# Where the activation buffers of a one-core decoder trunk begin, and a down projection in three passes

## The chip, the cores and the metric

One core of one Trainium2 chip runs the whole program. The metric is the device time of one execution in microseconds (us), taken as the median of several runs. The program has one launch and no communication with other cores.

## The reference

One decoder layer on 256 tokens of width 2048, in float32, with modulation vectors that come from a conditioning vector `c`. Cut to what matters:

```python
mod = silu(c) @ w_ada + b_ada                 # w_ada 2048 x 12288
sh1, sc1, g1, sh2, sc2, g2 = split(mod, 6)
h = rms_norm(x, norm_mix) * (1 + sc1) + sh1
proj = h @ w_in                               # "in":   2048 x 6656
mixed = concat(retention(proj), rwkv7(proj), moba_attention(proj))
x = x + g1 * (mixed @ w_out)                  # "out":  2048 x 2048
h = rms_norm(x, norm_ffn) * (1 + sc2) + sh2
u = causal_conv3(h @ w_up)                    # "up":   2048 x 11264
val, gate = split(u, 2)
x = x + g2 * ((silu(gate) * val) @ w_down)    # "down": 5632 x 2048
return rms_norm(x, norm_final)
```

The three mixers take little time beside the four projections; what bears on the change is the projections.

## The kernel before, in words

**Tiles and passes.** Activations lie transposed: features on the 128 partitions, the 256 tokens along the free dimension. Each float32 operand of a projection is split in two parts, `hi` (rounded to float32r) and `lo` (the rest). For each weight tile of 128 x 128 and each input tile of 128 features (a `k`), TensorE adds `whi*hi`, `whi*lo` and `wlo*hi` into a PSUM tile; the weight tile is the stationary operand and the activations are the moving one. "in", "out" and "up" do this in three passes of 256 columns (L1209, L1210, L1211). "down" (`WIDE`) does it in two: `whi` against `[hi | lo]` side by side, 512 columns into a whole PSUM bank (L1204), then `wlo*hi`, 256 columns into its first half (L1206). `evac_down` then adds both halves of the bank to the residual `x` (L1143, two operations).

**Counts.** A k of one output tile is one triplet of passes (a pair in "down"). "in" has 52 output tiles x 16 k = 832 triplets, "out" 16 x 16 = 256, "up" 88 x 16 = 1408, "down" 16 x 44 = 704. Of "up", 64 triplets (the first four k of 16 output tiles) run early, from `xg` (L1072 to L1082, 258 columns), while the norm before the MLP is still unknown, and are scaled by it later (L1095). The other 1344 triplets, 4032 matmuls, run from the normalized tiles `h` (L443 to L453).

**Weights.** SP's queue brings 1 MB (or 2 x 512 KB) `raw` buffers. Each holds two chunks of 8 weight tiles. ScalarE casts a chunk to `hi` (L471), VectorE subtracts to `lo` (L472), each of 128 x 1024. There are three buffers of each (`CONVB`), and `convert_until` runs two chunks ahead of the matmuls (`AHEAD`). Between the weights VectorE multiplies and sums 96 blocks of `w_ada` (L419, 128 x 2048 each), from the same raw buffers.

**Order.** The order of the weight tiles is a table (`weight_order`). The main loop goes over chunks: convert, hooks, eight triplets, evacuations, and some steps of the mixers' generators. A scheduler decides how the instructions that belong to different chunks are interleaved on each engine.

**The norm before "up".** After the last output tile of "out", the sum of squares (`acc`, L1061) goes through a matmul (`nps`, L1065), a short chain on VectorE that forms 1/sqrt by Newton steps (L385, L242 to L247, each on 128 x 2), a matmul that spreads it to all partitions (`rs`, L389) and a copy on ScalarE (`rs_ffn`, L399). With it the `h` tiles of "up" can be made. The last stretch of the kernel does the same with the final norm.

**Where buffers begin.** Activations that feed TensorE lie in the `arena` pool, 30 buffers of one tag. One buffer is `4T + 4` = 1028 floats, 4112 bytes, which the allocator rounds to 4128, and the pool begins at byte 31,104 of a partition. So the n-th buffer begins at 31104 + 4128 n, that is 384 + 32 n modulo 512: sixteen different places modulo 512. `pairs` puts hi and lo of two k into one buffer. The six converted weight buffers all begin at 320 modulo 512. These addresses are those of the built program.

```python
def piece(dt, name):                                              # L204
    return arena.tile([128, 4 * T + 4], dt, tag="s4", name=name)
```

Of the kernel before, what the change touches and what calls it, by code (L numbers as in the profile page):

```python
# [12 lines left out]
OP = mybir.AluOpType  # L13
# [155 lines left out]
WIDE = ("down",)  # L169
# [4 lines left out]
def trunk(tc, A):  # L174
# [254 lines left out]
    def split(g, sl, src):  # L429

        if g not in MX:
            MX[g] = pairs("mx")
        f, n, ts = sl
        while n:
            w = min(n, 2 - f % 2)
            x = MX[g][f // 2][:, f % 2:f % 2 + w]
            hi, lo = x[:, :, 0, ts], x[:, :, 1, ts]
            S.copy(hi, src[:, 0:w])
            V.tensor_tensor(lo, src[:, 0:w], hi.bitcast(F32), op=OP.subtract)
            src = src[:, w:]  # L440
            f, n = f + w, n - w

    def h_tile(kind, f):  # L443

        g, j = f // 4, f % 4
        if g not in H:
            H[g] = pairs("h")
        hi, lo = (H[g][j // 2][:, j % 2, i] for i in range(2))
        gain, shift = (mod[kind + n][:, f:f + 1] for n in ("_gain", "_shift"))
        xn = small.tile([128, T], F32, tag="xn", name=nm("xn"), bufs=2)  # L450
        V.scalar_tensor_tensor(xn, XN[kind][g][:, j], gain, RS[kind], op0=OP.mult, op1=OP.mult)
        S.activation(hi, xn, AF.Identity, bias=shift)
        V.scalar_tensor_tensor(lo, xn, shift, hi.bitcast(F32), op0=OP.add, op1=OP.subtract)  # L453
# [6 lines left out]
    def convert_until(c):  # L460
        while len(chunks) <= c and pos[0] < len(stream_items):
# [59 lines left out]
    def retention():  # L521
# [44 lines left out]
        for hh in range(2):  # L566
# [7 lines left out]
            split(0, (2 * hh, 2, slice(0, T)), mixed[:, 2 * hh:2 * hh + 2])  # L574
# [4 lines left out]
    def moba(h):  # L579
# [43 lines left out]
        split(g, (h % 4, 1, slice(0, T)), o[:, None, 0:256])  # L623
# [5 lines left out]
    def rwkv():  # L629
# [88 lines left out]
        R = [eighth(f"R{h}") for h in range(2)]  # L718
        vT, bT, kT = (half(n) for n in ("vT", "bT", "kT"))
# [61 lines left out]
        YV = half("yv")  # L781
# [78 lines left out]
        bd = [eighth(f"bd{h}") for h in range(2)]  # L860
# [49 lines left out]
        U = half("U")  # L910
# [4 lines left out]
        for h in range(2):  # L915
# [80 lines left out]
            split(1, (0, 4, sl), mixed[:, :, sl])  # L996
# [106 lines left out]
    def evac_up(t, part, ps):  # L1103
# [51 lines left out]
    def operands(m, k):  # L1155
# [3 lines left out]
        return src[k // 4][k % 4 // 2][:, k % 2]  # L1159
# [15 lines left out]
    for c in range(n_chunks):  # L1175
# [5 lines left out]
        for j in range(8):  # L1181
# [16 lines left out]
            ps = opened[t] if m in WIDE else opened[t][:, 0:T + 2] if early else opened[t][:, 0:T]  # L1198
            two = t in both
            opens = first and not (two and t % 2)  # L1200
# [96 lines left out]
```

## Time and profile before

| what | us |
|---|---|
| median of 3 runs | 1322.31 (1319.69 to 1325.14) |
| profiled execution, its own time | 1320.23 |
| span of its trace | 1318.3 |
| PE busy | 1269.5 (96%) |
| VectorE (DVE) busy | 1040.2 (79%) |
| ScalarE (ACT) busy | 651.1 (49%) |
| GpSimd (POOL) busy | 43.7 (3%) |
| mean granted TensorE clock | 0.987 |

The difference between the execution's own time and its span (1.9 us) is what lies outside the first and last instruction. A matmul of 256 columns is recorded with some 0.28 us, of which the larger part overlaps the next one; what a matmul costs in a row of them is the distance from its start to the start of the next, called its **pitch** below. It is read from the starts in the timeline, or from the length of a stretch and the count of matmuls in it. The stages, by the matmuls' lines: "in" 23 to 396.5 us, "out" 396.5 to 541.3, the early part of "up" to 583.3, "up" to 1057.0, "down" to 1302.7, the final norm and the last stores to 1318.4.

### The profile page before, as it was taken

What the parts mean: (1) busy time and instruction counts of PE and PEld (TensorE: products, weight loads), DVE (VectorE), ACT (ScalarE), POOL (GpSimd) and SP (SyncE); (2) the same over time, 40 slices, a digit from 0 to 9 for tenths busy, and PEclk for the clock granted to TensorE, in tenths of its full rate; (3) what the DMA queues carried; (4) which work ended last, traced back from release to release, by engine and by line L of the source; (5) the groups of instructions that cost most, each with busy time, mean ns of one, the idle gap of its engine ahead of it and who ended that gap; (6) DMA issues with size and microseconds to landing.
All of it is one profiled execution on the core that took longest, in us unless ns stands there. A gap on an engine that the chain in (4) does not pass through costs nothing.

```text
span 1318.3 us, 23905 instructions
## 1 busy us (share of the span) xinstructions
PE 1269.5 (96%) x9820; PEld 1219.6 (93%) x9820; DVE 1040.2 (79%) x1624; ACT 651.1 (49%) x1045; POOL 43.7 (3%) x41
## 2 busy tenths in 40 slices
PE   5899999999999999979999999999999999999995
PEld 5899999999999999979999999999999988888885
DVE  7888989999887579998776888898866766666544
ACT  3455445666345324456555656566555544444441
POOL 0000000000000001400000000000000000100000
PEclk8999999999999999989999999999999999999998
DMA  9999887785537269695864565565555666767551
GB/s 387 359 328 349 315 311 290 280 290 192 208 123 277 96 248 409 236 341 204 307 240 158 192 220 196 181 215 184 219 193 193 219 248 247 283 251 278 198 192 64
DMA packets 49934, 320.48 MB, mean 243 GB/s; under 512 B 5536, under 2 KB 6048, under 8 KB 15776
## 3 DMA queue, kind: packets, MB, share of 16 engines
q1 hardware_dynamic: 48528, 315.10, 65.1%
q0 software_dynamic: 1008, 3.67, 0.7%
q8 instruction: 77, 1.26, 0.4%
q14 instruction: 33, 0.27, 0.1%
q10 hardware_dynamic: 288, 0.17, 0.1%
HBM read 316.83 MB, written 2.10 MB: 242 GB/s over the span
## 4 chain that ended last, share of the span: by engine, by line
PE 55%; DVE 1%; ACT 0%; DVEq 0%; issue 0%; ACTq 0%
PE mm L1204 12%; PE mm L1209 12%; PE mm L1211 12%; PE mm L1210 12%; PE mm L1206 6%; DVE x L1151 0%; PE rs L389 0%; DVE x L1143 0%; DVEq L1292 0%; PE ms L1065 0%; DVE rsa L246 0%; DVE rsy L247 0%; DVE rsa L245 0%; DVE acc L1061 0%; ACT nsq L1060 0%
## 5 line engine op out<-in xcount | busy, mean ns | idle before, releaser
L472 DVE TENSOR_TENSOR lo<-raw,hi 128x1024 fp32r<-128x1024 f32 x400 | 489.2, 1225 | 194.7 <-ACT hi L471 192.5
L471 ACT CAST hi<-raw 128x1024 fp32r<-128x1024 f32 x400 | 419.5, 1050 | 436.7 <-PE mm L1210 248.3
L1209 PE MATMUL mm<-h,hi 128*128 128x256 f32 x2016 | 567.4, 282 | 0.7 <-ACT hi L471 0.6
L1211 PE MATMUL mm<-h,lo 128*128 128x256 f32 x2016 | 566.2, 281 | 1.1 <-DVE lo L472 1.1
L1210 PE MATMUL mm<-h,hi 128*128 128x256 f32 x2016 | 566.6, 281 | 0.0
L1211 PEld LDWEIGHTS mm<-h,lo 128*128 128x128 f32 x2016 | 379.9, 189 | 2.2 <-DVE lo L472 1.5
L1209 PEld LDWEIGHTS mm<-h,hi 128*128 128x128 f32 x2016 | 379.9, 188 | 1.8 <-ACT hi L471 0.8
L1210 PEld LDWEIGHTS mm<-h,hi 128*128 128x128 f32 x2016 | 379.7, 188 | 0.3
L1204 PE MATMUL mm<-g,hi 128*128 128x512 f32 x704 | 245.9, 394 | 0.0
L419 DVE SCALAR_TENSOR_TENSOR raw<-raw,cb 128x2048 f32<-128x2048 f32 x96 | 220.9, 2301 | 3.5 <-DMA raw<-w_ada 3.1
L1206 PE MATMUL mm<-g,lo 128*128 128x256 f32 x704 | 197.5, 281 | 0.0
L1204 PEld LDWEIGHTS mm<-g,hi 128*128 128x128 f32 x704 | 132.2, 188 | 30.3
L1206 PEld LDWEIGHTS mm<-g,lo 128*128 128x128 f32 x704 | 132.7, 188 | 0.0
L1209 PE MATMUL mm<-mx,hi 128*128 128x256 f32 x256 | 73.5, 287 | 1.2 <-DVE x L1047 1.2
L1210 PE MATMUL mm<-mx,hi 128*128 128x256 f32 x256 | 72.9, 285 | 0.0
L1211 PE MATMUL mm<-mx,lo 128*128 128x256 f32 x256 | 72.0, 281 | 0.5 <-DVE lo L472 0.5
L1061 POOL TENSOR_TENSOR acc<-acc,nsq 128x256 f32<-128x256 f32 x28 | 37.7, 1345 | 837.1 <-ACT nsq L1060 836.7
L1209 PE MATMUL pair<-h,hi 128*128 128x256 f32 x160 | 45.5, 296 | 7.0 <-ACT hi L471 5.1
L1209 PEld LDWEIGHTS mm<-mx,hi 128*128 128x128 f32 x256 | 48.2, 188 | 2.3 <-DVE x L1047 1.4
L1211 PEld LDWEIGHTS mm<-mx,lo 128*128 128x128 f32 x256 | 48.3, 189 | 0.6 <-DVE lo L472 0.6
L1210 PEld LDWEIGHTS mm<-mx,hi 128*128 128x128 f32 x256 | 48.2, 188 | 0.7 <-issue 0.2
L1210 PE MATMUL pair<-h,hi 128*128 128x256 f32 x160 | 46.0, 291 | 0.0
(290 smaller groups left out, 1222.7 us busy)
## 6 DMA issues: line engine op xcount, KB each, us to landing
raw<-w_ada SPq DMA_DIRECT2D x96, 1024.0 KB, 5.0
raw<-w_up SPq DMA_DIRECT2D x67, 1024.0 KB, 4.8
raw<-w_in SPq DMA_DIRECT2D x52, 1024.0 KB, 6.2
raw<-w_down SPq DMA_DIRECT2D x44, 1024.0 KB, 4.9
raw<-w_up SPq DMA_DIRECT2D x42, 512.0 KB, 8.7
raw<-w_out SPq DMA_DIRECT2D x18, 512.0 KB, 8.8
raw<-w_out SPq DMA_DIRECT2D x7, 1024.0 KB, 4.9
x<-xT SPq DMA_DIRECT2D x4, 512.0 KB, 5.5
```

The lines of the kernel that those rows point to most:

```text
L419: V.scalar_tensor_tensor(raw, raw, 1.0, cb, op0=OP.mult, op1=OP.mult, accum_out=m)
L471: S.copy(flat(hi), src)
L472: V.tensor_tensor(flat(lo), src, flat(hi).bitcast(F32), op=OP.subtract)
L1061: (V if t == NF - 1 else G).tensor_tensor(norm["acc"], norm["acc"], sq, op=OP.add)
L1204: PE.matmul(ps.rearrange("p (h t) -> p h t", h=2), whi[:, j], x, start=first, stop=False, skip_group_check=True)
L1206: PE.matmul(ps[:, 0:T], wlo[:, j], x[:, 0], start=False, stop=last, skip_group_check=True)
L1209: PE.matmul(ps, whi[:, j], hi, start=opens, stop=False, skip_group_check=two)
L1210: PE.matmul(ps, whi[:, j], lo, start=False, stop=False, skip_group_check=two)
L1211: PE.matmul(ps, wlo[:, j], hi, start=False, stop=last, skip_group_check=two)
```

## The change

1. An arena buffer is exactly 4T = 1024 floats, 4096 bytes, and a pad of `CONST_PAD` = 32 floats moves the pool's begin: in the built program the n-th buffer begins at 31232 + 4096 n, and all are at 0 modulo 512. The weight buffers stay at 320 modulo 512 (a pad of 80 floats in `stream` and one of 16 in `small` set this). The raw weight buffers move from 320 to 0 modulo 512.
2. `pairs` goes: a buffer now holds the hi parts of four k, another one the lo parts. `split` becomes one copy and one subtraction a call where it looped over pieces.
3. `WIDE` goes: "down" runs in three passes of 256 columns, and `evac_down` is one operation in place of two.
4. The first two groups of "down"'s input (8 of its 44 k) and `xg` lie in the `tail` pool, not in the arena. Their buffers are now 1056 floats; the four of them begin at 384, 0, 128 and 256 modulo 512. The early part of "up" still uses 258 columns out of rows of 4T + 8.

Numbers of matmuls by projection are unchanged but for "down", 704 x 3 in place of 704 x 2, with the same number of columns.

```diff
-WIDE = ("down",)
+CONST_PAD, SMALL_PAD = 32, 16
...
-    def piece(dt, name):
-
-        return arena.tile([128, 4 * T + 4], dt, tag="s4", name=name)
-
     def s4(name, dt=F32):
-        return piece(dt, nm(name))[:, 0:4 * T].rearrange("p (a b) -> p a b", a=4)
-
-    def pairs(name, tile_of=None):
-
-        shape = lambda x: x.rearrange("p (f h) t -> p f h t", h=2)
-        return [shape((tile_of or s4)(name, F32R)) for _ in range(2)]
+        return arena.tile([128, 4, T], dt, tag="s4", name=nm(name))
...
+    stream.tile([128, 80], F32, name="pad")
...
+    const.tile([128, CONST_PAD], F32, name="pad")
...
         if g not in H:
-            H[g] = pairs("h")
-        hi, lo = (H[g][j // 2][:, j % 2, i] for i in range(2))
+            H[g] = s4("hhi", F32R), s4("hlo", F32R)
+        hi, lo = H[g]
...
+    def gt_piece(name):
+
+        return tail[0].tile([128, 1056], F32R, tag="gt", name=name)
...
+    small.tile([128, SMALL_PAD], F32, name="pad")
...
-        hi, lo = (tail[0].tile([128, 4, T + 2], F32R, tag="gt", name=n) for n in ("xghi", "xglo"))
+        hi, lo = (gt_piece(n)[:, 0:4 * T + 8].rearrange("p (a b) -> p a b", a=4) for n in ("xghi", "xglo"))
...
-            GT[g] = pairs("g", first if g < 2 else s4)
+            GT[g] = (first("ghi"), first("glo")) if g < 2 else (s4("ghi", F32R), s4("glo", F32R))
...
     def evac_down(t, part, ps):
         dst = x1[t // 4][:, t % 4]
-        for h in range(2):
-            V.scalar_tensor_tensor(dst, ps[:, T * h:T * h + T], mod["g2"][:, t:t + 1], dst, op0=OP.mult, op1=OP.add)
+        V.scalar_tensor_tensor(dst, ps, mod["g2"][:, t:t + 1], dst, op0=OP.mult, op1=OP.add)
...
-            if m in WIDE:
-
-                x = operands(m, k)
-                PE.matmul(ps.rearrange("p (h t) -> p h t", h=2), whi[:, j], x, start=first, stop=False,
-                          skip_group_check=True)
-                PE.matmul(ps[:, 0:T], wlo[:, j], x[:, 0], start=False, stop=last, skip_group_check=True)
-            else:
-                hi, lo = (x[:, k] for x in XG) if early else (operands(m, k)[:, i] for i in range(2))
-                PE.matmul(ps, whi[:, j], hi, start=opens, stop=False, skip_group_check=two)
-                PE.matmul(ps, whi[:, j], lo, start=False, stop=False, skip_group_check=two)
-                PE.matmul(ps, wlo[:, j], hi, start=False, stop=last, skip_group_check=two)
+            PE.matmul(ps, whi[:, j], hi, start=first and not (two and t % 2), stop=False, skip_group_check=two)
+            PE.matmul(ps, whi[:, j], lo, start=False, stop=False, skip_group_check=two)
+            PE.matmul(ps, wlo[:, j], hi, start=False, stop=last, skip_group_check=two)
```

With the other buffer sizes the scheduler also interleaves VectorE's work differently. The place that matters is the chain of the norm before "up". VectorE, before, from the mean (`m`) to the result of the last Newton step (`rsy`); L472 is the weights' lo part, L419 a block of `w_ada` (`raw`), L421 and L427 finish the modulation vectors:

```order
L385 TENSOR_SCALAR m961_6234<-nps960_6231 128x2
...
L419 SCALAR_TENSOR_TENSOR raw993_6422,mod_ffn_shift_161<-raw993_6422,cb_97 128x2048
L245 SCALAR_TENSOR_TENSOR rsa963_6237<-rsy962_6236 128x2
...
L419 SCALAR_TENSOR_TENSOR raw1006_6503,mod_ffn_gain_162<-raw1006_6503,cb_97 128x2048
...
L419 SCALAR_TENSOR_TENSOR raw1028_6653,mod_ffn_shift_161<-raw1028_6653,cb_97 128x2048
...
L419 SCALAR_TENSOR_TENSOR raw1044_6734,mod_ffn_gain_162<-raw1044_6734,cb_97 128x2048
L247 SCALAR_TENSOR_TENSOR rsy962_6236<-rsa963_6237,rsy962_6236 128x2
L419 SCALAR_TENSOR_TENSOR raw1057_6811,mod_ffn_shift_161<-raw1057_6811,cb_97 128x2048
```

From `m` to the last `L247`, which is the one shown, the chain has four blocks of `w_ada` and five lo parts between its steps (the rows left out are lo parts and small steps); a fifth block follows it at once. VectorE, after, the same chain (now L379, L233 to L238; lo is L459, a block of `w_ada` L413):

```order
L379 TENSOR_SCALAR m961_6233<-nps960_6230 128x2
...
L413 SCALAR_TENSOR_TENSOR raw972_6320,mod_ffn_gain_164<-raw972_6320,cb_98 128x2048
L238 SCALAR_TENSOR_TENSOR rsy962_6235<-rsa963_6236,rsy962_6235 128x2
L459 TENSOR_TENSOR lo969_6285<-raw884_5680,hi968_6284 128x1024
L236 SCALAR_TENSOR_TENSOR rsa963_6236<-rsy962_6235 128x2
L459 TENSOR_TENSOR lo976_6327<-raw892_5746,hi975_6326 128x1024
...
L238 SCALAR_TENSOR_TENSOR rsy962_6235<-rsa963_6236,rsy962_6235 128x2
L459 TENSOR_TENSOR lo985_6372<-raw893_5747,hi984_6371 128x1024
```

Inside the chain stand one block of `w_ada` and two lo parts now; three blocks have moved behind it, and behind the first `h` tiles, as has the one that stood right after it. On TensorE the matmuls between `nps` and `rs` are those of the early part of "up": 101 before, 53 after.

TensorE in "down", before:

```order
L1204 MATMUL mm1883_13448<-g1368_9197,hi1876_13412 128x512
L1206 MATMUL mm1883_13448<-g1368_9197,lo1877_13413 128x256
L1204 MATMUL mm1883_13448<-g1369_9198,hi1876_13412 128x512
L1206 MATMUL mm1883_13448<-g1369_9198,lo1877_13413 128x256
L1204 MATMUL mm1883_13448<-g1413_9581,hi1881_13444 128x512
L1206 MATMUL mm1883_13448<-g1413_9581,lo1882_13445 128x256
```

and after:

```order
L1192 MATMUL mm1864_13614<-ghi1240_8152,hi1856_13536 128x256
L1193 MATMUL mm1864_13614<-glo1241_8153,hi1856_13536 128x256
L1194 MATMUL mm1864_13614<-ghi1240_8152,lo1857_13537 128x256
L1192 MATMUL mm1864_13614<-ghi1281_8480,hi1858_13564 128x256
L1193 MATMUL mm1864_13614<-glo1282_8481,hi1858_13564 128x256
L1194 MATMUL mm1864_13614<-ghi1281_8480,lo1859_13565 128x256
```

The wide pass is cut in two that read different buffers.

## Rows read from the trace of the kernel before

**Rows 1.** Stretches: length, busy us (count) PE, PEld, DVE, ACT, POOL; PEclk, DMA share, GB/s.

```profile
23.00:100.00 77.00, 70.83 (x552) 69.51 (x553) 65.54 (x78) 34.71 (x56) 0.00 (x0) 0.95 0.94 354
100.00:396.50 296.50, 294.38 (x2385) 285.32 (x2383) 272.62 (x509) 147.39 (x276) 3.67 (x5) 1.00 0.71 262
396.50:505.00 108.50, 107.46 (x861) 100.76 (x860) 76.28 (x147) 44.44 (x92) 2.20 (x4) 1.00 0.62 224
551.50:569.30 17.80, 12.90 (x106) 12.72 (x106) 17.15 (x32) 4.96 (x8) 0.00 (x0) 0.94 0.67 229
573.10:577.30 4.20, 4.17 (x19) 4.17 (x20) 2.97 (x6) 2.34 (x8) 0.00 (x0) 0.50 0.97 352
583.30:630.00 46.70, 46.70 (x396) 46.57 (x395) 39.96 (x48) 29.64 (x59) 0.00 (x0) 1.00 0.69 260
583.30:1057.00 473.70, 473.70 (x4035) 473.57 (x4034) 380.37 (x570) 270.26 (x412) 0.00 (x0) 1.00 0.59 212
1057.00:1302.70 245.70, 245.70 (x1410) 215.36 (x1408) 147.59 (x156) 104.53 (x119) 17.73 (x14) 1.00 0.62 227
```

**Rows 2.** Page, part 5: groups; count | busy us, mean ns | idle before, releaser.

```profile
L472 DVE TENSOR_TENSOR lo<-raw,hi 128x1024 fp32r<-128x1024 f32 x400 | 489.2, 1225 | 194.7 <-ACT hi L471 192.5
L471 ACT CAST hi<-raw 128x1024 fp32r<-128x1024 f32 x400 | 419.5, 1050 | 436.7 <-PE mm L1210 248.3
L419 DVE SCALAR_TENSOR_TENSOR raw<-raw,cb 128x2048 f32<-128x2048 f32 x96 | 220.9, 2301 | 3.5 <-DMA raw<-w_ada 3.1
```

**Rows 3.** Waits of ScalarE in 583.3 to 1057 us: total us, times, longest.

```profile
ACT hi L471 <- PE mm L1210: 138.4, 115, 1.8
```

**Rows 4.** Timeline of PE in "up": start us, us, engine, instruction.

```profile
802.63 0.28 PE L1209 MATMUL mm<-h,hi 128*128 128x256 f32 x1
803.31 0.28 PE L1209 MATMUL mm<-h,hi 128*128 128x256 f32 x1
804.03 0.28 PE L1209 MATMUL mm<-h,hi 128*128 128x256 f32 x1
804.74 0.28 PE L1209 MATMUL mm<-h,hi 128*128 128x256 f32 x1
```

**Rows 5.** Timeline of PE, early and late visits to one buffer in "up".

```profile
671.99 0.28 PE L1209 MATMUL mm<-h,hi 128*128 128x256 f32 x1
...
672.67 0.28 PE L1209 MATMUL mm<-h,hi 128*128 128x256 f32 x1
...
1054.85 0.28 PE L1209 MATMUL mm<-h,hi 128*128 128x256 f32 x1
...
1055.53 0.29 PE L1209 MATMUL mm<-h,hi 128*128 128x256 f32 x1
```

**Rows 6.** Timeline of PE in "out".

```profile
464.20 0.28 PE L1209 MATMUL mm<-mx,hi 128*128 128x256 f32 x1
...
464.91 0.28 PE L1209 MATMUL mm<-mx,hi 128*128 128x256 f32 x1
```

**Rows 7.** Timeline of PE in "down".

```profile
1099.89 0.39 PE L1204 MATMUL mm<-g,hi 128*128 128x512 f32 x1
1100.12 0.28 PE L1206 MATMUL mm<-g,lo 128*128 128x256 f32 x1
1100.24 0.39 PE L1204 MATMUL mm<-g,hi 128*128 128x512 f32 x1
```

**Rows 8.** Timeline of VectorE: the norm before "up", and the end of "down".

```profile
551.13 0.43 DVE L1061 TENSOR_TENSOR acc<-acc,nsq 128x256 f32<-128x256 f32 x1 [0.62 <-POOL acc L1061]
...
569.05 0.16 DVE L247 SCALAR_TENSOR_TENSOR rsy<-rsa,rsy 128x2 f32<-128x2 f32 x1
...
1303.01 1.00 DVE L1143 SCALAR_TENSOR_TENSOR x<-mm,mod_g,x 128x256 f32<-128x256 f32 x2 [6.17 <-PE mm L1206]
```

**Rows 9.** Waits of PE in 541.3 to 583.3 us: total us, times, longest.

```profile
PE rs L389 <- DVE rsy L247: 4.7, 1, 4.7
...
PE mm L1209 <- ACT silu_c L1110: 3.4, 2, 2.6
```

More of the change, by code (lines that the diff above doesn't have):

```diff
@@ L431, in split @@
         if g not in MX:
[L432 to L441, printed above, removed]
+            MX[g] = s4("mxhi", F32R), s4("mxlo", F32R)
+        hi, lo = (flat(x)[:, sl] if isinstance(sl, slice) else x[:, :, sl[0]] for x in MX[g])
+        S.copy(hi, src)
+        V.tensor_tensor(lo, src, hi.bitcast(F32), op=OP.subtract)
     def h_tile(kind, f):
@@ L467, in convert_until @@
                 half = half_of[0]
-                hi = stream.tile([128, 8, 128], F32R, tag="hi", name=nm("hi"), bufs=CONVB)
-                lo = stream.tile([128, 8, 128], F32R, tag="lo", name=nm("lo"), bufs=CONVB)
+                hi, lo = (stream.tile([128, 8, 128], F32R, tag=n, name=nm(n), bufs=CONVB) for n in ("hi", "lo"))
                 src = raw[half] if len(raw) == 2 else raw[0][:, 1024 * half:1024 * half + 1024]
@@ L573, in retention @@
             done()
-            split(0, (2 * hh, 2, slice(0, T)), mixed[:, 2 * hh:2 * hh + 2])
+            split(0, slice(512 * hh, 512 * hh + 512), flat(mixed[:, 2 * hh:2 * hh + 2]))
             yield 1 - hh
@@ L622, in moba @@
         yield
-        split(g, (h % 4, 1, slice(0, T)), o[:, None, 0:256])
+        split(g, slice(T * (h % 4), T * (h % 4) + T), o[:, 0:256])
         done()
@@ L633, in rwkv @@
         V.tensor_scalar(oka, vv("k_a", 0, 4), -1.0, 1.0, op0=OP.mult, op1=OP.add)
-        half = lambda name: piece(F32, name)[:, 0:1024].rearrange("p (a b) -> p a b", a=2)
-        eighth = lambda name: piece(F32, name)[:, 0:1024].rearrange("p (a b) -> p a b", a=8)
-        wua = half("wua")
+        wua = arena.tile([128, 2, 512], F32, tag="s4", name="wua")
         S.copy(wua[:, 0, 0:1], proj[3][:, 3, 0:1])
         G.dma_start(wua, A["wua"])
-        gup = half("gup")
+        gup = arena.tile([128, 2, 512], F32, tag="s4", name="gup")
         S.copy(gup[:, 0, 0:1], proj[3][:, 3, 0:1])
@@ L717, in rwkv @@
         PC = const.tile([128, 4, 8], F32, name="pc")
-        R = [eighth(f"R{h}") for h in range(2)]
-        vT, bT, kT = (half(n) for n in ("vT", "bT", "kT"))
+        R = [arena.tile([128, 8, 128], F32, tag="s4", name=f"R{h}") for h in range(2)]
+        vT, bT, kT = (arena.tile([128, 2, 512], F32, tag="s4", name=n) for n in ("vT", "bT", "kT"))
         c3 = lambda ap: ap.rearrange("p (h t) -> p h t", h=2)
@@ L780, in rwkv @@
         X = {}
-        YV = half("yv")
+        YV = arena.tile([128, 2, 512], F32, tag="s4", name="yv")
         mask = K("mask")
@@ L859, in rwkv @@
         ztv = zt.rearrange("p (i m s) -> p m s i", i=16, s=2)
-        bd = [eighth(f"bd{h}") for h in range(2)]
+        bd = [arena.tile([128, 8, 128], F32, tag="s4", name=f"bd{h}") for h in range(2)]
         for h in range(2):
@@ L908, in rwkv @@
             yield 1 - h
-        U = half("U")
+        U = arena.tile([128, 2, 512], F32, tag="s4", name="U")
         sb = mixer[0].tile([128, 4, 128], F32, name="sb")
@@ L995, in rwkv @@
             done()
-            split(1, (0, 4, sl), mixed[:, :, sl])
+            split(1, (sl,), mixed[:, :, sl])
             yield
@@ L1133, in evac_up @@
         if g not in GT:
-            first = lambda n, dt: tail[0].tile([128, 4, T], dt, tag="gt", name=nm(n))
-            GT[g] = pairs("g", first if g < 2 else s4)
-        hi, lo = (GT[g][j // 2][:, j % 2, i] for i in range(2))
-        S.copy(hi, v)
-        V.tensor_tensor(lo, v, hi.bitcast(F32), op=OP.subtract)
+            first = lambda n: gt_piece(nm(n))[:, 0:4 * T].rearrange("p (a b) -> p a b", a=4)
+            GT[g] = (first("ghi"), first("glo")) if g < 2 else (s4("ghi", F32R), s4("glo", F32R))
+        hi, lo = GT[g]
+        S.copy(hi[:, j], v)
+        V.tensor_tensor(lo[:, j], v, hi[:, j].bitcast(F32), op=OP.subtract)
     def evac_down(t, part, ps):
         dst = x1[t // 4][:, t % 4]
-        for h in range(2):
-            V.scalar_tensor_tensor(dst, ps[:, T * h:T * h + T], mod["g2"][:, t:t + 1], dst, op0=OP.mult, op1=OP.add)
+        V.scalar_tensor_tensor(dst, ps, mod["g2"][:, t:t + 1], dst, op0=OP.mult, op1=OP.add)
         norm_acc(t, dst)
@@ L1158, in operands @@
             k = RANK[k]
-        return src[k // 4][k % 4 // 2][:, k % 2]
+        hi, lo = src[k // 4]
+        return hi[:, k % 4], lo[:, k % 4]
     evac = {"in": evac_in, "out": evac_out, "up": evac_up, "down": evac_down}
@@ L1197, in trunk @@
             early = m == "up" and t % NP < EARLY and k < 4
[L1198 removed]
+            ps = opened[t][:, 0:T + 2] if early else opened[t][:, 0:T]
+            hi, lo = (x[:, k] for x in XG) if early else operands(m, k)
             two = t in both
[L1200 to L1211 removed]
+            PE.matmul(ps, whi[:, j], hi, start=first and not (two and t % 2), stop=False, skip_group_check=two)
+            PE.matmul(ps, whi[:, j], lo, start=False, stop=False, skip_group_check=two)
+            PE.matmul(ps, wlo[:, j], hi, start=False, stop=last, skip_group_check=two)
             if last:
```

4 lines of the change are left out of this document (2 added, 2 removed).

## The prediction

> **What bounds the kernel now.** I read the stretches first, then the waits, then the timeline of TensorE (PE), since only starts tell what a matmul costs. From 583.3 us to the end of "down" PE is busy for the whole length of both stretches, at clock 1.00, so at the upper of its two levels, 2.4 GHz [rows 1]. No transfer and no conversion is waited for there. ScalarE, on the contrary, waits 115 times for PE to give back a weight buffer [rows 3]: the converters stand as far ahead as the buffers let them. So what decides there is the distance from one matmul's start to the next, the pitch, alone. In "up" it is 473.70/4032 = 117.5 ns, in "down" 245.70/704 = 349.0 ns a pair [rows 1], which the timeline splits into some 0.23 for the 512 columns and 0.12 for the 256 [rows 7]. "in" has more holes, and VectorE is busy for 272.62 of 296.50 us of it, 92% [rows 1]. Before 100 us the DMA engines are busy for 0.94 of the time [rows 1], so loading sets the pace there.
>
> **What an address does.** In "up" the same 256-column matmuls come at two pitches. Follow the weight order to the buffer that each matmul reads. From 802.63 to 803.31 us six matmuls (two triplets) read an `h` buffer that the allocator put at byte 113,664, which is 0 modulo 512; the next six read one at 448 modulo 512, the six after that one at 192. The starts are 0.68, 0.72 and 0.71 us apart [rows 4]: 113, 120 and 118 ns each. The buffer at 0 is visited through all of "up", 528 matmuls in 88 visits; the first and the last visit take 0.68 us too, with other weights and at other DMA loads [rows 5]. Averaged over the 528, my own reading of all their starts gives 113.9 ns, nine in ten of them near 113. But a place at 0 isn't all of it: in "out" a buffer that also begins at 0 was read at 0.71 us for six, 118 ns [rows 6]. I read this as two levels, 113.3 and some 118, of which one holds until something disturbs it; places other than 0 show the higher one alone, or worse. With every buffer at 0 nothing in "up" throws the stream off between one buffer and the next, so I take 113.6: the low level, with one matmul in sixteen at 118. The bounds are 113.3 and 118.2.
>
> The rules I know speak against this. The Trainium skill ("TensorE: Matmul & The Clock Gate", Back-to-back issue gap) gives the distance of an isolated matmul as columns/2.4 + 2.5 ns at the full clock: 109.2 for 256, 215.8 for 512, and has no term for where an operand begins; the skill ("SBUF — State Buffer", Who interferes with whom) gives the moving operand and the weights independent read ports and says that PE waits for no one. By these the change would bring nothing in "up" and cost 704 x 2.6 ns = 1.8 us in "down". The trace disagrees on the address, with 113 and 120 ns for one shape within 2 us; it is a rival below all the same.
>
> **The change part by part**, against the profiled execution, 1320.2 us:
>
> - "up": 4032 x (117.5 - 113.6) = **-15.7 us** (113.3: -16.9; 118.2: +2.8).
> - "in" from 100 us on: 2496 matmuls of the projection less 552 before it [rows 1], 1944, at some 118 now. All at 113.6 would give 1944 x 4.5 = 8.7 us. I take half, **-4.5**: the mixers' matmuls and waits break the stream, after which the higher level holds for a while, and VectorE at 92% can't go much faster (bounds 0 and -9). Before 100 us 0, because the transfers set the pace (at best 552 x 4.5 = -2.5).
> - "out": 768 x 4.5 = 3.5 at most; **-1.5**, since the one buffer at 0 stood on the higher level there [rows 6].
> - "down": 36 of 44 k come from the arena, at 0: 576 x 3 x 113.6 = 196.3 us. 8 k come from the tail pool, where one buffer in four is at 0: 128 x 3 x 117.5 = 45.1. Sum 241.4 for 245.7, **-4.3**. The bounds are 704 x 3 x 113.3 = 239.3 (-6.4) and, at 118.2, 249.6 (+3.9). So three narrow passes win only at the lower level: two passes of 256 at 113.6 are 227 ns for the 231 or so of one of 512; at 118.2 they are 236.
> - The start of "up": VectorE's chain runs from 551.6 (`acc` ends) to 569.2 (`rsy` ends), 17.6 us [rows 8]. The new order takes three blocks of `w_ada` at 2.30 and three lo parts at 1.225 [rows 2] out of it, 10.6 us, which leaves 7.0. PE has 53 early matmuls to cover it, 53 x 0.12 = 6.4 us, where 101 were not enough: it waited 4.7 us for the result [rows 9]. The 48 matmuls that are now behind `rs` give work while the first `h` tiles are made, where it waited 3.4 for ScalarE's copies [rows 9]; and after these waits the clock was 0.50, the 1.2 GHz level, for 4.20 us, in which 19 matmuls took 220 ns each and not 120, 1.9 us more [rows 1]. In all 10.0 us are at stake; I take half, **-5** (0 to -10). The moved blocks, four with the one behind the chain, 9.2 us, go to a VectorE that in 583 to 630 has 46.70 - 39.96 = 6.7 us free [rows 1]. They fit only if spread a little beyond it; what a lump of them would cost is a rival.
> - The end: the last output tile's two operations take 1.00 us [rows 8]; one is left, **-0.5**. For the other 15 tiles, as for `split`, VectorE's saving lies beside matmuls that don't wait for it: 0. The lost side-by-side reading of hi and lo costs nothing beyond its passes, which are counted. Raw buffers at another place: the conversions that read them have a lead, 0.
>
> Sum: -15.7 - 4.5 - 1.5 - 4.3 - 5 - 0.5 = -31.5, so 1288.7. The median of the runs is 2.1 above the profiled execution, which makes 1290.8; I say **1290**.
>
> **The rivals.**
>
> - *The address is not what counts, or the higher level holds.* Then "up" is at 118.2, +2.8, "down" +3.9, "in" and "out" 0; the norm's chain still gives -5 and the end -0.5: 1320.2 + 1.2 = 1321, with the 2.1 some 1323, no change; 1319 if it is 117.8. For it: rows 6, and that the low level was only ever seen in short visits. Against it: 88 visits out of 88 different surroundings showed it, first and last alike [rows 5], and nothing in the new stream is different from a visit that goes on. Chance 0.12.
> - *VectorE becomes the bound.* In "up" it works 380.37 us [rows 1]; in 458 us that is 83%, and the stretch with the moved blocks is full. If "in", "out" and the norm give nothing and "up" gives 10 of its 15.7, it is 1320.2 - 10 - 4.3 - 0.5 + 2.1 = 1307 or so. For it: 92% in "in". Against it: ScalarE's 115 waits for PE [rows 3]. Chance 0.10.
> - *Slower.* One mechanism: the four moved blocks run one after the other in front of a lo part, behind which PE stands. Converters are at most two chunks ahead, 2 x 24 x 0.1175 = 5.6 us, of which their own 1.05 + 1.225 [rows 2] leave 3.4. A lump of 9.2 us beyond that lead makes PE wait 5.8, and such a hole puts the stream on the higher level, where "up" (+2.8) and "down" (+3.9) stay. With -5 and -0.5 from the norm and the end: 1320.2 + 7.0 + 2.1 = 1329. It decides if the lump is over 3.4 us and the higher level doesn't fall back by itself. Against it: in the trace the buffer at 0 was found at the low level again at each visit. Chance 0.03.
>
> **How the numbers follow.** My forecast has 0.75, the rivals 0.12, 0.10 and 0.03. The forecast by itself goes from all ends at their best (-16.9 - 9 - 2.5 - 3.5 - 6.4 - 10 - 0.5 = -49; not all at once: I take -43, 1279) to "in", "out" and the norm at nothing (-20.5, 1302). The range has to leave out no more than 0.2: it takes in the second rival, and a part of "up" at the higher level beyond it, 1277 to 1313, and leaves out the first and the third. 0.5% of this kernel, 6.6 us, is about what a measurement can tell from no change. Forecast and second rival are faster by more, 0.85, with a small part of the first one 0.86; no change 0.11; slower 0.03.
>
> **What would show it.** Right: PE starts 0.68 us apart for six matmuls in "up" nearly everywhere; the "up" stage some 458 us long and "down" 241; in "down" the k from the tail pool at 117 or more, the rest at 113; one block of `w_ada` within the norm's chain, and that chain about 7 us. Wrong: a uniform 118 in "up", which makes "down" 249 us; PE waits for L459 after 583 us; a stage "in" as long as before with VectorE close to 100%.

## The result and the profile after

The changed kernel takes 1282.14 us (median of 4 runs, 1280.55 to 1284.61), the kernel before beside it 1323.72: a ratio of 0.9704, 95% interval 0.9686 to 0.9721. The forecast was 1290, in a range of 1277 to 1313. The profiled execution took 1284.61 us with a span of 1282.8, so 35.6 us less than the profiled one of before. Of the nine runs of the changed kernel in all, and of the four of `e6_both_by_64`, the ratios leave out one each, 1309.58 and 1307.57 us; what the trace of the first shows stands under `e10_changed_again`.

The profile after gives the loss stage by stage. The stretches are cut at the starts of the first matmul of "out", the last one of "out", the first of "up" from `h`, and the first and last of "down".

| stretch | before | after | change | forecast |
|---|---|---|---|---|
| "in" | 373.5 | 369.7 | -3.8 | -4.5 |
| "out" | 150.6 | 151.7 | +1.1 | -1.5 |
| last of "out" to first of "up" | 36.1 | 25.4 | -10.7 | -5 |
| "up" | 473.7 | 457.0 | -16.7 | -15.7 |
| "down" | 245.7 | 240.8 | -4.9 | -4.3 |
| the end | 15.7 | 14.9 | -0.8 | -0.5 |
| sum | | | -35.8 | -31.5 |

The same stretches as in [rows 1], after (length; busy us and counts of PE, PEld, DVE, ACT, POOL; PE clock, DMA share, GB/s):

```profile
23.20:100.00 76.80, 70.91 (x572) 69.54 (x573) 66.54 (x80) 36.24 (x59) 0.00 (x0) 0.94 0.95 360
100.00:392.90 292.90, 290.43 (x2364) 280.66 (x2363) 271.26 (x508) 146.19 (x273) 3.66 (x5) 1.00 0.72 264
...
434.60:438.00 3.40, 3.40 (x26) 2.87 (x24) 1.71 (x3) 0.27 (x1) 0.00 (x0) 1.00 0.65 263
438.00:441.40 3.40, 3.40 (x17) 2.85 (x17) 0.57 (x2) 1.28 (x4) 0.00 (x0) 0.50 0.02 10
...
541.80:570.10 28.30, 26.16 (x215) 25.59 (x214) 26.11 (x47) 17.91 (x49) 5.36 (x4) 1.00 0.69 259
570.10:617.00 46.90, 46.90 (x416) 46.90 (x415) 46.16 (x55) 29.64 (x55) 0.00 (x0) 1.00 0.74 262
570.10:1027.10 457.00, 457.00 (x4035) 457.00 (x4034) 389.48 (x584) 269.89 (x406) 0.00 (x0) 1.00 0.65 226
1027.10:1267.90 240.80, 240.80 (x2113) 240.80 (x2112) 141.01 (x141) 103.14 (x119) 15.14 (x14) 1.00 0.65 232
```

"up" is 457.0/4032 = 113.3 ns a matmul; in my own reading of its starts 4031 of the 4032 matmuls are at the lower level, 113 to 114 ns. In the timeline two places of the changed kernel, one in "up" and one in "in", show how evenly each level runs (where [rows 4] had 113, 120 and 118 side by side):

```profile
801.98 0.28 PE L1192 MATMUL mm<-hhi,hi 128*128 128x256 f32 x1
...
802.66 0.28 PE L1192 MATMUL mm<-hhi,hi 128*128 128x256 f32 x1
...
803.34 0.28 PE L1192 MATMUL mm<-hhi,hi 128*128 128x256 f32 x1
```

```profile
199.74 0.28 PE L1192 MATMUL mm<-hhi,hi 128*128 128x256 f32 x1
...
200.44 0.28 PE L1192 MATMUL mm<-hhi,hi 128*128 128x256 f32 x1
...
201.15 0.28 PE L1192 MATMUL mm<-hhi,hi 128*128 128x256 f32 x1
```

Six matmuls take 0.68 us in the first and 0.71 in the second, from buffers of the same place. "in" stands on the higher level for most of its length: by my reading 548 of 1862 undisturbed matmuls from 100 us on are at the lower one, 1298 at 117 or more. So the address alone doesn't give the lower level; it makes it possible. "In" also gained at another place than it seems: 572 of its matmuls had started by 100 us where it was 552 before, and by the starts the first 552 took 2.6 us less and the other 1944 only 1.3 us less.

In "out" stands something that the kernel before has not: from 438.0 to 441.4 us the clock is 0.50, the 1.2 GHz level, right after a stretch of the same length in which PE had no gap. Half the clock for 3.4 us costs some 1.7 us (an estimate). In the traces of `e6_both_by_64`, `e8_nudges` and `e11_four_nudges`, whose "out" stays at 1.00, it takes 149.5 to 149.9 us; in those of `e4_wide_down_aligned`, `e7_weights_at_64` and `e10_changed_again`, with nearly 7 us at 0.50, 152.8 to 153.5.

The chain before "up" (as [rows 8]), VectorE's timeline after:

```profile
547.93 0.43 DVE L1046 TENSOR_TENSOR acc<-acc,nsq 128x256 f32<-128x256 f32 x1 [0.62 <-POOL acc L1046]
...
550.00 2.28 DVE L413 SCALAR_TENSOR_TENSOR raw<-raw,cb 128x2048 f32<-128x2048 f32 x1
...
555.40 0.16 DVE L238 SCALAR_TENSOR_TENSOR rsy<-rsa,rsy 128x2 f32<-128x2 f32 x1
```

and the waits of PE there (as [rows 9]; total us, times, longest), 541.8 to 570.1 us:

```profile
PE mm L1192 <- DVE x L1032: 1.0, 1, 1.0
PE nps L1050 <- DVE acc L1046: 1.0, 1, 1.0
...
PE rs L383 <- DVE rsy L238: 0.2, 1, 0.2
```

The chain takes 7.2 us (548.36 to 555.56) for 17.6; PE's wait for its result is 0.2 us for 4.7, the wait for ScalarE's copies is gone, and so is the stretch at the 1.2 GHz level that followed them: the row 541.8 to 570.1 stands at 1.00. The moved blocks of `w_ada` fill VectorE to 46.16 of 46.90 us in the row 570 to 617. No wait of PE stands in the trace from 570 us to the end of "down". At the end one operation of 0.48 us is left of two:

```profile
1268.22 0.48 DVE L1133 SCALAR_TENSOR_TENSOR x<-mm,mod_g,x 128x256 f32<-128x256 f32 x1 [5.97 <-PE mm L1194]
```

### The profile page after: what moved, and what is told of

Its sections match the earlier page's. It is cut to its first block, busy times and chain, and to the rows that moved or that the text cites. A ratio compares the mean times of both kernels' runs of the same rounds, so it can differ in the third digit from the quotient of the medians.

```text
span 1282.8 us, 25320 instructions
## 1 busy us (share of the span) xinstructions
PE 1242.3 (97%) x10524; PEld 1222.0 (95%) x10524; DVE 1031.6 (80%) x1606; ACT 650.6 (51%) x1043; POOL 39.9 (3%) x41
## 4 chain that ended last, share of the span: by engine, by line
PE 89%; DVE 7%; issue 2%; ACT 1%; DMA 0%; POOL 0%; DVEq 0%; ACTq 0%; POOLq 0%
PE mm L1192 26%; PE mm L1194 26%; PE mm L1193 26%; DVE raw L413 2%; DVE lo L459 2%; PE pair L1194 1%; PE pair L1192 1%; PE pair L1193 1%; PE xx L778 1%; PE u L915 1%; PE sp L923 1%; PE sp L937 1%; PE akv L788 1%; PE yps L917 0%; ACT hi L458 0%
## 5 line engine op out<-in xcount | busy, mean ns | idle before, releaser
L459 DVE TENSOR_TENSOR lo<-raw,hi 128x1024 fp32r<-128x1024 f32 x400 | 488.4, 1224 | 161.0 <-ACT hi L458 158.2
L1192 PE MATMUL mm<-hhi,hi 128*128 128x256 f32 x2016 | 560.2, 278 | 0.2
L1194 PE MATMUL mm<-hhi,lo 128*128 128x256 f32 x2016 | 559.4, 278 | 0.7 <-DVE lo L459 0.7
L1193 PE MATMUL mm<-hlo,hi 128*128 128x256 f32 x2016 | 559.5, 278 | 0.0
L1194 PEld LDWEIGHTS mm<-hhi,lo 128*128 128x128 f32 x2016 | 379.2, 188 | 1.7 <-DVE lo L459 1.3
L1192 PEld LDWEIGHTS mm<-hhi,hi 128*128 128x128 f32 x2016 | 379.1, 188 | 1.3 <-issue 0.3
L1193 PEld LDWEIGHTS mm<-hlo,hi 128*128 128x128 f32 x2016 | 378.8, 188 | 0.3
L413 DVE SCALAR_TENSOR_TENSOR raw<-raw,cb 128x2048 f32<-128x2048 f32 x96 | 221.3, 2305 | 10.4 <-DMA raw<-w_ada 9.6
L1192 PE MATMUL mm<-ghi,hi 128*128 128x256 f32 x704 | 194.8, 277 | 0.0
L1193 PE MATMUL mm<-glo,hi 128*128 128x256 f32 x704 | 194.8, 277 | 0.0
L1194 PE MATMUL mm<-ghi,lo 128*128 128x256 f32 x704 | 194.8, 277 | 0.0
L1192 PEld LDWEIGHTS mm<-ghi,hi 128*128 128x128 f32 x704 | 132.2, 188 | 0.0
```

The lines of the kernel that those rows point to most:

```text
L413: V.scalar_tensor_tensor(raw, raw, 1.0, cb, op0=OP.mult, op1=OP.mult, accum_out=m)
L459: V.tensor_tensor(flat(lo), src, flat(hi).bitcast(F32), op=OP.subtract)
L1192: PE.matmul(ps, whi[:, j], hi, start=first and not (two and t % 2), stop=False, skip_group_check=two)
```

## The experiments

The change has three parts that touch the time: the places, the passes of "down", and the order around the norm. The first four kernels and `e9_split_alone` take each of them alone or away. Rows in this section are stretches as above, "up" or "down" of the kernel named.

**`e1_align_alone`** (in the kernel before):

```diff
-        return arena.tile([128, 4 * T + 4], dt, tag="s4", name=name)
+        return arena.tile([128, 4 * T], dt, tag="s4", name=name)
...
+    stream.tile([128, 80], F32, name="pad")
...
+    const.tile([128, 32], F32, name="pad")
```

> The kernel before with its arena buffers put at 0 modulo 512 and nothing else: hi and lo of two k still share a buffer, down still has its 512-column pass, the norm chain before up keeps its four blocks of w_ada. Theory A (the place of the moving operand against the weights sets the pitch): up 457 us in place of 473.7, a low-level pitch of 113 to 114; down about 241 (576 pairs at some 227 + 113.5 ns, 128 at 349); in and out together 3 to 5 us shorter; the chain before up as before, 17 to 18 us. Time about 1297 (1292 to 1302). If up falls to the higher level by chance, 475 us and about 1318. Rival B (the gain came with the new order and the separate hi and lo buffers): up 473.7 and 1322, within 4.

Measured: 1300.49, 1300.72, 1303.32 and 1319.41 us, ratio 0.9879 (0.9815 to 0.9943). The profiled run is the last one:

```profile
578.60:1053.70 475.10, 474.93 (x4034) 474.73 (x4033) 380.69 (x570) 270.04 (x412) 0.00 (x0) 1.00 0.59 212
1053.70:1302.00 248.30, 248.30 (x1409) 215.97 (x1409) 147.60 (x156) 104.53 (x119) 17.92 (x14) 1.00 0.61 225
```

"up" is at 117.7 there. Its timeline tells where that began; the bracket is the idle time and what ended it:

```profile
584.21 0.28 PE L1211 MATMUL mm<-h,hi 128*128 128x256 f32 x1
584.65 0.38 PE L1212 MATMUL mm<-h,lo 128*128 128x256 f32 x1 [0.17 <-DVE lo L473]
584.87 0.28 PE L1210 MATMUL mm<-h,hi 128*128 128x256 f32 x1
```

Before it the pitch was 113; from then on it is 118 to the end of "up". The level turned at one wait of 0.17 us for a lo part that came late. That the other three runs, 16 to 19 us shorter, had the lower level in "up" fits 4032 x 4.4 = 18 us, but isn't shown: there is no trace of them. They lie 3 to 6 us above the expected 1297, which counted on 241 us for "down"; `e4_wide_down_aligned` bears on that.

**`e2_stride_4128`** (in the changed kernel):

```diff
-        return arena.tile([128, 4, T], dt, tag="s4", name=nm(name))
+        return arena.tile([128, 4 * T + 4], dt, tag="s4", name=nm(name))[:, 0:4 * T].rearrange("p (a b) -> p a b", a=4)
...
-    stream.tile([128, 80], F32, name="pad")
...
-        return tail[0].tile([128, 1056], F32R, tag="gt", name=name)
+        return tail[0].tile([128, 1032], F32R, tag="gt", name=name)
```

(the other arena tiles likewise, and no pads in `const` and `small`).

> The changed kernel with the arena buffers at a stride of 4128 bytes again, so at sixteen places modulo 512; separate hi and lo buffers, three passes in down and the new order stay. Theory A: up 474 (within 3), down 704 x 3 x 117.7 = 248.6, the stretch from the end of out to up some 9 us shorter than before, the end 0.5: about 1317 (1312 to 1321). Rival B: up 457 and about 1283.

Measured: 1318.80 us, 0.9975 (0.9966 to 0.9985). "up" 477.6, "down" 249.6, the stretch before "up" 25.4. Without the places nearly all of the gain is gone, though order and passes stay: theory A. The 10.7 us before "up" are still there, but "up" and "down" are each 3.9 us longer than in the kernel before. Being at the good place now and then isn't enough either: here the hi parts and the lo parts lie at different places modulo 512, so the matmuls alternate between them, and of 704 matmuls of "up" that read a buffer at 0 only one was at 113 to 114.

**`e3_three_passes_alone`** (in the kernel before): `WIDE = ()`, and one operation in `evac_down`.

> The kernel before with down in three passes of 256 columns and nothing else. Theory A: passes read at 117.7 ns on average, 353 a triplet for 349 a pair: down 248.6 in place of 245.7, less 0.5 at the end: 1326 (1323 to 1329). Rival C (three narrow passes are faster by themselves): down 241 or less, 1318.

Measured: 1324.16 us, 1.0022 (1.0012 to 1.0032). "down" went from 245.7 to 249.7.

**`e4_wide_down_aligned`** (in the changed kernel): "down" as before, hi and lo of two k in one buffer at 0, the 512-column pass and the two operations back.

> The changed kernel with down in two passes again (512 columns, hi and lo side by side in one buffer at 0 modulo 512, and 256). Theory A: at the aligned place the wide pass takes some 227 ns and the narrow one 113.5, so 576 x 340.5 + 128 x 349 = 240.8, and the time is that of the changed kernel within 2 us, 1281 to 1285 with the second operation of the end. Rival C: down 245.7 as before, 1287.

Measured: 1292.35 us, 0.9770 (0.9751 to 0.9790), 10 us above the changed kernel's 1282.14 (5 above the 1287.02 of its second set, below), and 9.1 by the spans of the two traces, 1291.9 and 1282.8. Theory A missed here: "up" is at the lower level, but "down" isn't:

```profile
570.00:1028.00 458.00, 457.52 (x4034) 457.14 (x4033) 389.48 (x584) 270.07 (x406) 0.00 (x0) 1.00 0.63 226
1028.00:1276.40 248.40, 248.40 (x1409) 215.87 (x1408) 147.68 (x156) 104.50 (x119) 17.47 (x14) 1.00 0.62 225
```

The narrow pass took 118.3 ns and the wide one 234.7 on average, from the first pair of "down" on. "down" in its four combinations:

| "down", us | two passes | three passes |
|---|---|---|
| sixteen places | 245.7 | 249.7 |
| 0 modulo 512 | 248.4 | 240.8 |

Each part alone makes it longer; together they save 4.9. Each of the four is one trace.

**`e5_weights_at_0`, `e6_both_by_64`, `e7_weights_at_64`** (in the changed kernel; one of these lines each):

```diff
-    stream.tile([128, 80], F32, name="pad")
+    pass
```

```diff
-CONST_PAD, SMALL_PAD = 32, 16
+CONST_PAD, SMALL_PAD = 48, 16
```

```diff
-    stream.tile([128, 80], F32, name="pad")
+    stream.tile([128, 16], F32, name="pad")
```

> The changed kernel without the pad of 80 floats ahead of the weight buffers: they begin at 0 modulo 512 in place of 320; the arena stays at 0. Theory A (the distance between moving operand and weights modulo 512 sets the pitch, and 192 is a good one): at distance 0 the kernel before ran its 256-column passes at 117.5 to 118, so up 475 (472 to 480) and down 249, time 1309 (1304 to 1315). Rival D (what counts is that the moving operand begins at 0 modulo 512, wherever the weights are): up 457, 1282.

> The changed kernel with a pad of 48 floats in place of 32 ahead of the arena: arena buffers at 64 modulo 512, weight buffers at 384, the distance still 192. Theory A: as the changed kernel, up 457 and 1282; 1301 if up falls to the higher level. Rival D: up 475 and about 1309.

> The changed kernel with a pad of 16 floats ahead of the weight buffers in place of 80: they begin at 64, the distance is 448 modulo 512. In the kernel before the up matmuls at this distance took 116.4 on average, a quarter of them 113. Theory A with a period of 256: a low level again, up 457 to 462, 1282 to 1288 (1301 to 1306 at the higher one). Theory A with 192 alone: up about 470, down 247, 1302. Rival D: 1282.

Measured: `e5_weights_at_0` 1331.69 us, 1.0068 (1.0041 to 1.0094); `e6_both_by_64` 1285.23, 0.9714 (0.9680 to 0.9747), with one run at 1307.57 of which there is no trace; `e7_weights_at_64` 1283.23, 0.9714 (0.9682 to 0.9746). "up" of the three, in this order:

```profile
575.70:1059.50 483.80, 483.80 (x4034) 483.80 (x4033) 391.76 (x584) 267.80 (x406) 0.00 (x0) 1.00 0.62 214
```

```profile
566.60:1024.20 457.60, 457.22 (x4034) 457.03 (x4033) 389.34 (x584) 270.05 (x406) 0.00 (x0) 1.00 0.66 226
```

```profile
569.60:1026.60 457.00, 457.00 (x4035) 457.00 (x4034) 389.54 (x584) 270.67 (x406) 0.00 (x0) 1.00 0.65 226
```

The arena at 0 with the weights at 0 gives 483.8/4032 = 120.0 ns, slower than the mixture of before, and dearer than expected; the arena at 64 with the weights at 384 gives 113.5, a wait of 0.38 us included (shown under `e10_changed_again`). Rival D is refuted: the activations at 0 alone don't give the lower level. The distance between the two fits all three runs, with 192 and 448 good and 0 bad; other distances weren't made uniform. One rival stays untested: that weights at 0 are bad by themselves, whatever the distance, since no run has them there with activations elsewhere. What speaks for the distance is that in the kernel before the weights stay at 320 and the pitch still goes with the place of the activations [rows 4].

**`e8_nudges`** and **`e11_four_nudges`** (in the changed kernel, behind the third pass; the second one with four of them in a row):

```diff
+            if m == "up" and c % 8 == 4 and j == 3 and not early:
+                PE.matmul(ybank("nudge")[0:128, 0:4], whi[:, j], hi[:, 0:4], start=True, stop=True)
```

> The changed kernel with 21 small extra matmuls of 4 columns in up, one every eighth chunk, into a PSUM bank that nothing reads. Theory E (two levels that hold themselves until something disturbs the stream): some of the 21 throw the stream to the other level, where it stays until the next at least, so up shows whole stretches of 8 chunks (192 matmuls, 22 us) at 118 and others at 113; with half of each 467 us, time about 1292, differing from run to run. Rival F (the place alone sets the level, a disturbance is over at once): up 457 + 21 x 0.1 = 459, 1284.

Measured: 1303.96 us, 0.9874 (0.9840 to 0.9907). The stretches from one nudge to the next, the first five:

```profile
577.28:600.01 22.73, 22.73 (x196) 22.73 (x194) 21.21 (x25) 14.48 (x26) 0.00 (x0) 1.00 0.62 207
600.01:622.73 22.72, 22.72 (x195) 22.72 (x194) 19.30 (x26) 12.81 (x22) 0.00 (x0) 1.00 0.95 370
622.73:645.46 22.73, 22.73 (x196) 22.73 (x195) 18.71 (x20) 11.02 (x18) 0.00 (x0) 1.00 0.77 275
645.46:667.35 21.89, 21.89 (x195) 21.89 (x194) 20.51 (x26) 10.01 (x15) 0.00 (x0) 1.00 0.88 316
667.35:690.07 22.72, 22.72 (x195) 22.72 (x194) 12.12 (x15) 11.52 (x16) 0.00 (x0) 1.00 0.58 210
```

Each holds 192 matmuls of the projection. 0.84 us of difference over 192 is 4.4 ns each: the two levels, held for whole stretches, whatever VectorE and the DMA share do in them. The lower level came back behind the 4th, 8th, 12th, 16th and 20th nudge and behind no other. Theory E had said that each stretch keeps one level, but with half of the stretches at each and 1292 us; five of 21 at the lower one made 1304. `e11_four_nudges` asked whether four at once close such a cycle.

> The kernel with nudges, with four small matmuls at each of the 21 places in place of one. With one, the level came back to 113 behind the 4th, 8th, 12th, 16th and 20th and was 118 behind all others, so a nudge moves the stream one step in a cycle of four, one of which is the low level. Theory G (that cycle): four at once close the cycle, all stretches stay at 113, up 457 + 21 x (0.1 to 0.46) = 459 to 467, time 1284 to 1292. Rival J (each disturbance throws it anew, with one chance in four): three quarters of the stretches at 118, up 473 or more, 1303.

Measured: 1319.28 us, 0.9978 (0.9965 to 0.9991). "up" is 483.8 us, of which the 84 small matmuls take some 9; behind the first group every stretch is at 118. Theory G failed: four at once aren't four single ones. Rival J had the bound right (473 or more) and not the mechanism: a level drawn anew each time would have been the lower one behind some of the 21 groups. What a disturbance does to the level isn't settled; that the level then holds is.

**`e9_split_alone`** (in the kernel before; the reads of "out" follow the new layout, not shown):

```diff
-        f, n, ts = sl
-        while n:
...
+        f, n, ts = sl
+        hi, lo = (x.rearrange("p f h t -> p (f h) t")[:, f:f + n, ts] for x in MX[g])
+        S.copy(hi, src)
+        V.tensor_tensor(lo, src, hi.bitcast(F32), op=OP.subtract)
```

> The kernel before with split in one copy and one subtraction a call, and nothing else: buffers at their sixteen places, hi and lo in one buffer, wide down. Built, VectorE's order in the norm chain before up is that of the changed kernel: one block of w_ada inside it. Theory H (the order makes the gain at the start of up): from the last matmul of out to the first of up 25.4 us in place of 36.1, all other stages as before: about 1311 (1308 to 1314). Rival I (it comes from the new xg buffers, or is given back in up): 36 us or up longer, 1321.

Measured: 1310.84 us, 0.9915 (0.9896 to 0.9935). Its VectorE timeline before "up":

```profile
550.46 0.42 DVE L1056 TENSOR_TENSOR acc<-acc,nsq 128x256 f32<-128x256 f32 x1 [0.62 <-POOL acc L1056]
...
552.52 2.29 DVE L419 SCALAR_TENSOR_TENSOR raw<-raw,cb 128x2048 f32<-128x2048 f32 x1
...
557.92 0.16 DVE L247 SCALAR_TENSOR_TENSOR rsy<-rsa,rsy 128x2 f32<-128x2 f32 x1
```

The chain takes 7.2 us, the stretch from "out" to "up" 25.4. A simplification of `split`, far from the norm, moved the scheduler's order and gave 10.7 us by itself.

**`e10_changed_again`**: the changed kernel, unedited.

> The changed kernel once more, for how often up falls to the higher level. Of the 20 runs of aligned kernels without nudges so far (the changed one, both by 64, weights at 64, wide down, alignment alone) 2 were 18 us or more above the others of their kernel. Theory E: median 1282, with none to two of the runs at 1300 to 1308 (up at 476, and down at 248 behind it). Rival: the changed kernel's start is always at the lower level, all within 1280 to 1287.

Measured: 1287.02 us, 0.9729 (0.9710 to 0.9748): four runs from 1284.92 to 1287.17 and one of 1309.58, of which the trace is. Its "up" ran at 113 for the first 890 matmuls; then PE and VectorE, in this order:

```profile
673.69 0.28 PE L1193 MATMUL mm<-hlo,hi 128*128 128x256 f32 x1
674.21 0.38 PE L1194 MATMUL mm<-hhi,lo 128*128 128x256 f32 x1 [0.25 <-DVE lo L459]
```

```profile
670.72 2.29 DVE L413 SCALAR_TENSOR_TENSOR raw<-raw,cb 128x2048 f32<-128x2048 f32 x1 [1.12 <-DMA raw<-w_ada]
672.94 0.08 DVE L413 DVE_READ_ACCUMULATOR raw<-raw,cb 128x1 f32 x1
672.94 1.22 DVE L459 TENSOR_TENSOR lo<-raw,hi 128x1024 fp32r<-128x1024 f32 x1
```

The two parts of "up":

```profile
572.90:674.00 101.10, 101.06 (x892) 100.86 (x890) 91.72 (x109) 55.65 (x95) 0.00 (x0) 1.00 0.81 287
674.00:1044.30 370.30, 370.09 (x3142) 370.09 (x3143) 298.90 (x476) 212.67 (x312) 0.00 (x0) 1.00 0.59 201
```

VectorE waited 1.12 us for a block of `w_ada`, the lo part queued behind that block came 0.25 us late, and from there to the end of "up" 3,142 matmuls took 370.30 us, 117.9 each; "down" stood on the higher level too, 248.5 us. A wait of the same kind stood at the turn of `e1_align_alone`. The mean granted clock of this run, 0.986, is within that of the other four, 0.986 to 0.988, so the clock isn't the reason.

But such a wait doesn't always turn the level. `e6_both_by_64` has a longer one in "up", behind a block of `w_ada` as well, and stays at 113: its other 3,380 matmuls take 383.0 us, 113.3 each.

```profile
640.15 0.28 PE L1193 MATMUL mm<-hlo,hi 128*128 128x256 f32 x1
640.80 0.38 PE L1194 MATMUL mm<-hhi,lo 128*128 128x256 f32 x1 [0.38 <-DVE lo L459]
```

```profile
641.20:1024.20 383.00, 383.00 (x3381) 383.00 (x3381) 322.59 (x505) 226.21 (x330) 0.00 (x0) 1.00 0.63 215
```

`e4_wide_down_aligned` and `e12_tail_aligned` have one of 0.47 us each for a lo part too, up to 644.59 and 641.46 us, and stay. So in five traces with a late lo part in "up" the level turned twice (0.17 and 0.25 us) and stayed three times (0.38, 0.47, 0.47); what decides isn't shown.

**`e12_tail_aligned`** (in the kernel of `e7_weights_at_64`): the tail pool in two tags of two buffers, 1024 and 1088 floats, and `SMALL_PAD` 48, so that its buffers lie at distances 192 and 448.

> The kernel with the weights at 64 (distance 448), with the four buffers of the tail pool also at distance 448 or 192, so all 44 k of down lie at one of the two good places. Theory A: the 384 matmuls of down on tail buffers, 117.5 ns in the changed kernel, go to 113.5: down 240.8 - 1.5 = 239.3, and the time 1281 to 1282, some 1.5 below the same kernel without it. Rival: changing between 192 and 448 breaks the level, down 241 or more.

Measured: 1281.63 us, 0.9698 (0.9676 to 0.9719).

```profile
1024.80:1264.00 239.20, 239.20 (x2113) 239.20 (x2112) 141.34 (x141) 103.18 (x119) 15.14 (x14) 1.00 0.65 234
```

"down" is 239.2 us, 113.3 a matmul, as forecast. The 1.6 us are clear in the trace and too small for the times.

A change of place by itself doesn't wipe the level out. In the changed kernel "down" goes sixteen times from the tail's buffers (24 matmuls) to the arena's (108); the first two rounds:

```profile
1027.06:1029.87 2.81, 2.81 (x26) 2.81 (x25) 1.60 (x2) 1.51 (x2) 0.00 (x0) 1.00 0.78 239
1029.87:1042.12 12.25, 12.25 (x111) 12.25 (x109) 8.46 (x12) 5.88 (x7) 0.00 (x0) 1.00 0.76 287
1042.12:1044.93 2.81, 2.81 (x26) 2.81 (x25) 2.81 (x3) 1.35 (x3) 0.00 (x0) 1.00 0.32 61
1044.93:1057.18 12.25, 12.25 (x111) 12.25 (x109) 6.95 (x8) 4.62 (x6) 0.00 (x0) 1.00 0.79 296
```

That is 117 ns on the tail's buffers and 113.4 behind them, each time. In `e10_changed_again`, which comes into "down" on the higher level, the same rounds take 2.82 and 12.72 us, 117.8 behind them, each time too.

## Why the prediction was right, and where not

**The bound, and what an address does: right.** After 583 us the pitch alone decided, and "up" came to 113.3 ns for a forecast of 113.6. The two runs that settle it have the same program but for one pad: `e5_weights_at_0` at 120.0, `e7_weights_at_64` at 113.3. The place of the weights counts as well, most likely through the distance; the forecast spoke of 0 modulo 512 alone, since in the kernel before the weights lay at one place and the two couldn't be told apart. The rules that were weighed don't cover this: the formula of the Trainium skill ("TensorE: Matmul & The Clock Gate", Back-to-back issue gap) for an isolated matmul works out at 109.2 ns for 256 columns (an estimate) and has no term for where an operand begins. The runs show 113.3, 118 and 120 at one shape, one clock and one order.

One support of the forecast was misread. It says that 88 visits of 88 to the buffer at 0 showed the lower level. In its trace 78 did; from 947 us on every second visit, ten in all, stood at 117.7, here the six matmuls of the first:

```profile
947.30 0.28 PE L1209 MATMUL mm<-h,hi 128*128 128x256 f32 x1
...
948.01 0.28 PE L1209 MATMUL mm<-h,hi 128*128 128x256 f32 x1
```

Nor is it right that other places show the higher level alone: at the place 256, distance 448, 204 of 528 matmuls of "up" were at 113 or so. So the first rival had more for it than the forecast saw, and that a uniform stream would be on the lower level and mostly stay there its rows couldn't tell: that part was luck.

**"Holds until something disturbs it": right, with a wrong cost.** I wrote that the higher level "holds for a while" and took one matmul in sixteen there. In the runs neither level falls back by itself: "up" had 4031 of 4032 at the lower one, "in" long stretches on the higher one. The terms for "in" (-3.8 for -4.5) and "out" (+1.1 for -1.5) rest on that: half of "in" was a guess at how often the mixers' matmuls and waits leave it high. That it came out near is luck: of the 3.8 us, 2.6 come from the first 552 matmuls, where the forecast took 0, and 1.3 from the rest, where it took 4.5. In "out" 189 of 768 matmuls were at the lower level, and the stretch at the 1.2 GHz level, which the forecast didn't have, cost some 1.7 us; without such a stretch `e6_both_by_64` has 149.5 us, -1.1.

**"down": the size right, for one reason more than I gave.** 240.8 for 241.4, with 117.5 on the tail's buffers. The forecast weighed the passes by their columns alone, two of 256 at 113.6 against one of 512 at 231; `e4_wide_down_aligned` shows that with a wide pass in the stream the lower level isn't there at all, though "up" ended on it. So the three passes aren't a small gain beside the places, but the condition for it: 7.6 us of "down" hang on them.

**The start of "up": the term mis-sized.** Of 10.0 us at stake I took half, and 10.7 came. The chain's 7.0 us (7.2 measured) was right; the mistake was to doubt that 53 + 48 early matmuls cover it. They do, and then no wait stands there, so no clock step follows it either.

**The rivals.** The first (the higher level holds) named a thing that happens, with too general a condition: the one run of nine of the changed kernel that was over 20 us longer went to the higher level in "up" at one moment. The second (VectorE as the bound) is refuted: "up" at 457 us with VectorE busy 389.48 of it. The third named the place and the cause well, a late lo part behind moved blocks of `w_ada` whose hole puts the stream on the higher level, but not its size: the hole is 0.25 us where I priced 5.8, the loss is the level behind it, and with the places and the norm's gain the kernel is still faster than before. It happened in one run of nine here, in one of four of `e1_align_alone`, whose order of blocks is the old one, and by its time perhaps in one of four of `e6_both_by_64`; three traces have the hole and not the loss.

**The 7.9 us between the forecast's 1290 and the median.** By the table the stages came out 4.3 us shorter than forecast, with 5.7 at the start of "up" and smaller misses both ways. The forecast also put the median 2.1 us above the profiled execution, and here it lies 2.5 below it. The second set of runs of the same kernel has its median at 1287.02, 4.9 us higher, so a part of the miss is no more than two sets differ by.

## What to carry to other kernels

Read the pitch of matmuls from their starts, by the buffer that they read, before taking a PE-bound stage as done: one shape can have several. Where a place runs faster, make the whole stream uniform, and look for single short waits within it: one of a quarter of a microsecond stood at the start of a loss of over 20 us here, though three longer ones cost no more than themselves. Giving the lo parts more lead in "up" is the next thing to try and wasn't tried. And look at the order of the instructions after any edit: one that was meant to tidy a copy moved 10 us.

## What the hardware showed that was not expected

- The same stream of 256-column matmuls with weight loads runs at 113.3 ns or at 118, for hundreds of microseconds each, at the distance 192 modulo 512. At 448 it ran at 113.3 all through "up", and with activations and weights both at 0 at an even 120.0.
- The level is carried through matmuls at other distances: sixteen times through 24 matmuls on the tail's buffers, back to 113.4 in the changed kernel and to 117.8 in `e10_changed_again`.
- A single extra matmul of 4 columns can change the level: in `e8_nudges` the first one did, and the lower level came back behind every fourth; four in a row never brought it back. A late lo part turned it in two traces and not in three. What the level depends on inside the engine stays open.
- With 512-column passes between the narrow ones the stream at distance 192 ran at 118.3 and 234.7 ns all through "down", and was slower than at sixteen mixed places.
